# Recurrence gates from one stacked operand tile: a rounded half and its rest in the rows, both gates in the columns

## The chip, the cores and the metric

The kernel runs on one core of a Trainium2 chip. The metric is the device time of one execution in microseconds. Five engines work side by side, each through its own queue in order: TensorE (PE; its weight loads are shown apart as PEld), VectorE (DVE), ScalarE (ACT), GpSimd (POOL) and SyncE (SP), which issues the transfers here.

## What is computed

One layer of a hybrid decoder trunk on 2048 tokens of width 1024. A normalised input is projected to two groups that run side by side: four HGRN2 heads (a chunked gated recurrence with 128x128 states) and an RG-LRU group of width 512. Their outputs are concatenated, projected back and added to the input; a SwiGLU feed-forward part and a last norm follow. The part that the change touches is the RG-LRU group:

```python
def rglru_mix(xb, gate_b, conv_w, conv_b, wa, ba, wx, bx, a_param):
    ...
    xblk = xc.reshape(B, S, LRU_BLOCKS, LRU_BLOCK_DIM)
    r = jax.nn.sigmoid(jnp.einsum('bsnd,nde->bsne', xblk, wa.astype(jnp.float32)).reshape(B, S, W) + ba)
    ig = jax.nn.sigmoid(jnp.einsum('bsnd,nde->bsne', xblk, wx.astype(jnp.float32)).reshape(B, S, W) + bx)
    log_a = -LRU_C * r * jax.nn.softplus(-a_param.astype(jnp.float32))
    a = jnp.exp(log_a)
    b_in = jnp.sqrt(-jnp.expm1(2.0 * log_a)) * (ig * xc)
```

`xc` is the convolved input, 8 blocks of 64 channels. Both gates are block-diagonal: each block of 64 channels has its own 64x64 matrix in `wa` (recurrence gate `r`) and in `wx` (input gate `ig`).

## The kernel before

The sequence is worked in two halves of 1024 tokens, each in two blocks (`c` = 0, 1) of 512 tokens. Channels lie on the 128 partitions and tokens in the 512 columns. Large products run in a rounded 32-bit format; to keep the accuracy, both sides are split into a rounded part (`hi`, a ScalarE cast) and the rest (`lo`, a VectorE subtraction), and three matmuls hi·hi, lo·hi and hi·lo are added in PSUM (`feat_mm`, L234 to L236; `split`, L207 and L208).

After the values, a loop over eight steps `s` takes two weight slices and, for both blocks, makes two projections `pa` and `pb` of 24 matmuls each. Even steps feed one head of the HGRN2 group: `hg_pre` (`sf`, `lg`, `b`, the exponentials, the tiles `W`, `QI`, `K`), later `hg_mid` (transposes `pk`, scores `pc`), `hg_state` (`pu` and the four states `S`) and `hg_post` (`po`). Odd steps feed one unit of 128 channels, that is two blocks of 64, of the RG-LRU group: `lru_pre` (the convolution into `xc`, and its split `xh`, `xl`), then `lru_gates` (two PSUM banks `pr` and `pi`, three matmuls each against the gate weights `gwh` and `gwl`), then `lru_sigmoids` (`r`, `ig`, and the tanh `t`). The exponential, the root and the scan of a unit follow with the next even step's work (`exps`, `ends`). Names end in step and block: `pr_1_0` is the gate bank of step 1 (unit 0), block 0. The trace leaves these numbers out.

The gate weights are a 128x128 block-diagonal matrix for each unit and gate: half of its entries are zeros.

Two things set the order. Hooks in the loop (L1009 and on) place the later parts of a unit a number of projections behind; and the framework's scheduler then orders each engine's queue by a time line of its own. So small parts (`pk`, `pc`, `pu`, `po`, the gates) lie interleaved between the projections' matmuls on TensorE. A waiting instruction holds up all that stands behind it on its engine. There are four PSUM banks for projections and four for the small parts.

The feed-forward stage follows, with matmuls of 512 columns into `quad` banks and then the down projection.

Of the kernel before, what the change touches and what calls it, by code (L numbers as in the profile page):

```python
# [9 lines left out]
F32R = mybir.dt.float32r  # L10
# [8 lines left out]
NU = 4  # L19
# [9 lines left out]
NPAIR = NF // 2  # L29

C_LB0, C_LB1, C_CONVW, C_CONVB, C_BA, C_BX, C_A, C_NW, C_HN = 0, 4, 8, 24, 28, 32, 36, 40, 48
N_COLS = 49


@with_exitstack
def hybrid_layer(ctx: ExitStack, tc: tile.TileContext, x, x_t, norm_w, cols, w_in, gate_w, w_out, w_gu, w_down, out):
# [10 lines left out]
    def page(nm, dt=F32):  # L47
        return sb.tile([P, CW], dt, tag="pg", name=nm, bufs=16)
# [20 lines left out]
    def aux(nm):  # L69
        return psp.tile([P, CW], F32, tag="aux", name=nm)  # L70
# [192 lines left out]
    def table_act(out, in_, func, **kw):  # L263
        need = TABLES.get(func, at["table"])
        if need != at["table"]:
            in_line(lambda: nc.scalar.preload_act_table(func))
            at["table"] = need
        in_line(lambda: nc.scalar.activation(out=out, in_=in_, func=func, **kw))
# [145 lines left out]
    def lru_pre(u, psx, psg, nm):  # L414
        xp = sb.tile([P, CW + 4], F32, tag="pg", name="xp" + nm, bufs=16)
        v.tensor_copy(out=xp[:, 0:3], in_=hist[:, u, :])
        nc.scalar.copy(out=xp[:, 3 : 3 + CW], in_=psx)
        nc.gpsimd.tensor_copy(out=hist[:, u, :], in_=xp[:, CW : CW + 3])
        gl = page("gl" + nm)
        table_act(gl, psg, AF.Gelu_apprx_tanh)  # L420
        xc = page("xc" + nm)

        def cw(k):
            return par[:, C_CONVW + k * 4 + u : C_CONVW + k * 4 + u + 1]

        v.tensor_scalar(
            out=xc, in0=xp[:, 0:CW], scalar1=cw(0), scalar2=par[:, C_CONVB + u : C_CONVB + u + 1], op0=ALU.mult, op1=ALU.add
        )
        for k in range(1, 4):
            v.scalar_tensor_tensor(out=xc, in0=xp[:, k : k + CW], scalar=cw(k), in1=xc, op0=ALU.mult, op1=ALU.add)  # L430
        xh, xl = page("xh" + nm, dt=F32R), page("xl" + nm, dt=F32R)
        split((xh, xl), xc)
        return gl, xc, xh, xl


    def lru_gates(u, r, nm):
        gl, xc, xh, xl = r["pre"]
        r["p"] = pr, pi = aux("pr" + nm), aux("pi" + nm)
        for m, pg in enumerate((pr, pi)):
            gs = slice((m * NU + u) * P, (m * NU + u + 1) * P)  # L440
            nc.tensor.matmul(pg, lhsT=gwh[:, gs], rhs=xh, start=True, stop=False)
            nc.tensor.matmul(pg, lhsT=gwl[:, gs], rhs=xh, start=False, stop=False)
            nc.tensor.matmul(pg, lhsT=gwh[:, gs], rhs=xl, start=False, stop=True)

    def lru_sigmoids(u, d, nm):
        xc, (pr, pi) = d["pre"][1], d["p"]
        r, ig, t = d["r"] = xin("r" + nm), xin("ig" + nm), late("t" + nm)
        table_act(r, pr, AF.Sigmoid, bias=par[:, C_BA + u : C_BA + u + 1])
        table_act(ig, pi, AF.Sigmoid, bias=par[:, C_BX + u : C_BX + u + 1])
        table_act(t, r, AF.Tanh, scale=msp[:, u : u + 1])  # L450
        v.tensor_tensor(out=ig, in0=ig, in1=xc, op=ALU.mult)

# [720 lines left out]
def _layout(i):  # L1173
    import numpy as np

    a = {k: np.asarray(t) for k, t in i.items()}
    W = 512

    def by_rows(w):
        n = w.shape[1] // W  # L1180
        w = w.reshape(4, 2, P, n, W).transpose(3, 0, 2, 1, 4)
        return w.reshape(n * 4, P, D)

    def by_cols(w):
        n = w.shape[1] // P
        return w.reshape(KT, P, n, P).transpose(2, 1, 0, 3).reshape(n, P, D)

    w = a["w_in"][0]
    q, f_, v_, g_, lx, lg = (w[:, j * W : (j + 1) * W] for j in range(6))
    units = [by_rows(v_)]  # L1190
    for j in range(4):
        s = slice(j * P, (j + 1) * P)
        units += [by_cols(t[:, s]) for t in (q, f_, lx, lg)]
    units.append(by_rows(g_))

    def col(t):
        return t.reshape(-1, 4, P).transpose(2, 0, 1).reshape(P, -1)

    cols = [col(t) for t in (a["hg_lb"], a["conv_w"][0], a["conv_b"], a["lru_ba"], a["lru_bx"], a["lru_a"])]
    cols = np.concatenate(cols + [a["mix_norm_w"][0].reshape(KT, P).T, a["hg_norm_w"][0][:, None]], axis=1)  # L1200
    gate_w = np.zeros((P, 2, NU, P), np.float32)
    for m, t in enumerate((a["lru_wa"][0], a["lru_wx"][0])):
        for b in range(8):
            o = (b % 2) * 64
            gate_w[o : o + 64, m, b // 2, o : o + 64] = t[b]
    return {
        "x": a["x"][0],
        "x_t": a["x"][0].T,
        "norm_w": np.stack([a["mix_norm_w"][0], a["ffn_norm_w"][0], a["final_norm_w"]]),
        "cols": cols,  # L1210
        "w_in": np.concatenate(units, axis=0),
        "gate_w": gate_w.reshape(P, D),
        "w_out": by_rows(a["w_out"][0]),
        "w_gu": by_cols(a["w_gate_up"][0]),
        "w_down": a["w_down"][0].reshape(NF, P, D),
    }
# [19 lines left out]
```

## Time and profile before

| | us |
|---|---|
| median of 3 runs | 2115.37 |
| lowest and highest | 2114.73, 2115.42 |
| the profiled execution | 2114.84 |
| its span, first to last instruction | 2113.1 |

The profile is that of one execution. Its page gives the busy time of each engine and the chain of work that ended last; queries of its trace give groups of instructions, windows and a time line. TensorE's clock was granted at 0.999 over the span. What an engine that waits costs can be read only where TensorE or the last chain waits for it. By the windows the first 100 us hold 92.5 us of TensorE time, the window from 800 to 900 us 97.9, and all others up to 2100 us are full.

### The profile page before, as it was taken

The numbers are of one execution on the slowest core, as the hardware profiler recorded it, in microseconds if no ns is written. First come the engines' busy times: TensorE is split into PE (matmuls) and PEld (weight loads), VectorE is DVE, ScalarE is ACT, GpSimd is POOL, SyncE is SP. The second block draws the span as 40 slices with busy tenths as digits, with TensorE's granted clock in tenths as the row PEclk, the third lists the DMA queues.
The fourth block names the chain that finished last, engine by engine and source line by source line (L and its number), as shares of the span: only waits on it lengthen the run. The fifth ranks groups of instructions, "written<-read, shape, count | busy, mean of one in ns | idle before, by whom it ended". The sixth has DMA issues, their size and how long they took to land.

```text
span 2113.1 us, 26109 instructions
## 1 busy us (share of the span) xinstructions
PE 2096.0 (99%) x9704; PEld 1735.4 (82%) x9704; DVE 1485.9 (70%) x2415; ACT 959.0 (45%) x1608; POOL 77.0 (4%) x130
## 2 busy tenths in 40 slices
PE   8999999999999999999999999999999999999998
PEld 6888888888888887888888888888888888888887
DVE  5577765636777566877676669878867667669787
ACT  5566654535666554533333344335333333334333
POOL 2000001100000000000000000000000000000000
PEclk9999999999999999999999999999999999999999
DMA  5111115841111167423232266335423223267424
GB/s 210 51 41 41 41 40 183 293 140 52 39 33 40 42 224 233 152 93 125 95 109 97 89 238 217 120 133 189 145 95 130 95 95 110 95 222 247 155 85 145
DMA packets 138420, 262.84 MB, mean 124 GB/s; under 512 B 11186, under 2 KB 27570, under 8 KB 138292
## 3 DMA queue, kind: packets, MB, share of 16 engines
q1 hardware_dynamic: 138292, 261.17, 36.8%
q8 instruction: 76, 1.25, 0.2%
q14 instruction: 52, 0.43, 0.1%
HBM read 197.95 MB, written 63.18 MB: 124 GB/s over the span
## 4 chain that ended last, share of the span: by engine, by line
PE 97%; DMA 2%; DVE 1%; ACT 0%; issue 0%; SPq 0%; POOL 0%; DVEq 0%; POOLq 0%; ACTq 0%
PE quad_g L654 11%; PE quad_a L654 11%; PE quad_e L654 11%; PE pda L925 10%; PE pdb L925 7%; PE quad_f L654 6%; PE pb L235 3%; PE pb L236 3%; PE pa L235 3%; PE pa L234 3%; PE pa L236 3%; PE pb L234 3%; PE poh L246 2%; PE poh L247 2%; PE poh L248 2%; PE pg L248 1%
## 5 line engine op out<-in xcount | busy, mean ns | idle before, releaser
L654 PE MATMUL quad_f<-act_f,wgu_f 128*128 128x512 f32 x528 | 128.7, 393 | 1.9 <-ACT wgu_c L207 1.9
L654 PE MATMUL quad_a<-act_a,wgu_a 128*128 128x512 f32 x528 | 127.7, 390 | 0.2 <-DVE h L1114 0.2
L654 PE MATMUL quad_a<-act_b,wgu_b 128*128 128x512 f32 x528 | 127.1, 390 | 0.0
L654 PE MATMUL quad_g<-act_g,wgu_g 128*128 128x512 f32 x528 | 127.0, 390 | 0.0
L654 PE MATMUL quad_e<-act_e,wgu_e 128*128 128x512 f32 x528 | 126.9, 390 | 0.0
L654 PE MATMUL quad_e<-act_c,wgu_c 128*128 128x512 f32 x528 | 126.9, 390 | 0.0
L654 PE MATMUL quad_g<-act_d,wgu_d 128*128 128x512 f32 x528 | 126.8, 389 | 0.0
L654 PEld LDWEIGHTS quad_f<-act_f,wgu_f 128*128 128x128 f32 x528 | 100.2, 190 | 23.2 <-ACT act_g L207 2.3
L538 DVE TENSOR_TENSOR u<-u,quad_g 128x512 f32<-128x512 f32 x88 | 60.5, 688 | 79.7 <-PE quad_g L654 79.7
L654 PEld LDWEIGHTS quad_a<-act_a,wgu_a 128*128 128x128 f32 x528 | 98.9, 188 | 21.0 <-ACT act_c L207 0.6
L654 PEld LDWEIGHTS quad_e<-act_c,wgu_c 128*128 128x128 f32 x528 | 99.2, 188 | 20.6
L654 PEld LDWEIGHTS quad_g<-act_d,wgu_d 128*128 128x128 f32 x528 | 99.2, 188 | 20.5
L654 PEld LDWEIGHTS quad_g<-act_g,wgu_g 128*128 128x128 f32 x528 | 99.1, 188 | 20.5
L654 PEld LDWEIGHTS quad_e<-act_e,wgu_e 128*128 128x128 f32 x528 | 99.1, 188 | 20.5
L654 PEld LDWEIGHTS quad_a<-act_b,wgu_b 128*128 128x128 f32 x528 | 99.1, 188 | 20.5
L236 PE MATMUL pa<-xn,whi_in 128*128 128x512 f32 x256 | 100.9, 394 | 0.0
L234 PE MATMUL pa<-xn,whi_in 128*128 128x512 f32 x256 | 100.8, 394 | 0.0
L235 PE MATMUL pb<-xn,wlo_in 128*128 128x512 f32 x256 | 100.8, 394 | 0.0
L236 PE MATMUL pb<-xn,whi_in 128*128 128x512 f32 x256 | 100.7, 393 | 0.0
L235 PE MATMUL pa<-xn,wlo_in 128*128 128x512 f32 x256 | 100.5, 392 | 0.0
L234 PE MATMUL pb<-xn,whi_in 128*128 128x512 f32 x256 | 100.0, 391 | 0.0
L247 PE MATMUL poh<-wlo_o,mx 128*128 128x512 f32 x256 | 99.4, 393 | 0.0
(323 smaller groups left out, 4879.9 us busy)
## 6 DMA issues: line engine op xcount, KB each, us to landing
raw<-in_w_gu SPq DMA_DIRECT2D x88, 512.0 KB, 3.8
raw_in<-in_w_in SPq DMA_DIRECT2D x48, 512.0 KB, 3.5
ao_p<-as SPq DMA_DIRECT2D x76, 256.0 KB, 2.6
raw_o<-in_w_out SPq DMA_DIRECT2D x32, 512.0 KB, 4.1
x<-in_x SPq DMA_DIRECT2D x32, 256.0 KB, 5.7
xrh<-in_x SPq DMA_DIRECT2D x32, 256.0 KB, 3.6
h<-h SPq DMA_DIRECT2D x32, 256.0 KB, 3.4
hn<-hths SPq DMA_DIRECT2D x32, 256.0 KB, 3.7
```

Source lines behind the costliest of these rows:

```text
L234: nc.tensor.matmul(ps, lhsT=whi[:, ks], rhs=hi, start=(k == 0), stop=False)
L235: nc.tensor.matmul(ps, lhsT=wlo[:, ks], rhs=hi, start=False, stop=False)
L236: nc.tensor.matmul(ps, lhsT=whi[:, ks], rhs=lo, start=False, stop=(k == KT - 1))
L246: nc.tensor.matmul(ps, lhsT=hi, rhs=whi[:, ks], start=(k == 0), stop=False)
L247: nc.tensor.matmul(ps, lhsT=hi, rhs=wlo[:, ks], start=False, stop=False)
L248: nc.tensor.matmul(ps, lhsT=lo, rhs=whi[:, ks], start=False, stop=(k == KT - 1))
L538: (e or v).tensor_tensor(out=out, in0=a, in1=b, op=op)
L654: nc.tensor.matmul(ps, lhsT=w[:, s, ks], rhs=x, start=first and k + n == 0, stop=k == 3 and n == 2, skip_group_check=not first)
L925: nc.tensor.matmul(ps, lhsT=x, rhs=y, start=first and q + n == 0, stop=q == gr.n - 1 and n == 2, skip_group_check=not first)
```

## The change

A unit's 128 channels are two blocks of 64. The new `lru_pre` makes two operand tiles. In `za` rows 0 to 63 (`LO`) hold the rounded first block and rows 64 to 127 (`HI`) its rest; in `zb` rows 64 to 127 hold the rounded second block and rows 0 to 63 its rest. The gate weights are laid out anew: for each block of 64 channels the 64x64 matrices of both gates stand side by side in 128 columns, and the same 64 rows are repeated below. One matmul then multiplies the rounded part and the rest by the same weights and adds both, for both gates at once. With the rounded weights and with their rest this takes two matmuls a block of 64 channels, four a unit and token block, where six were. The products are those of before and one more (rest by rest).

Each PSUM bank now holds both gates of 64 channels, so `lru_sigmoids` empties it in halves: four sigmoids of 64 partitions in place of two of 128. For `ig` the result goes to the other half of the partitions; four more parameter columns hold `bx` with its halves exchanged. The two casts and two subtractions of `lru_pre` work on 64 partitions each, and the subtractions write to the other half.

```diff
+C_BXS = 49
+N_COLS = 53
+LO, HI = slice(0, P // 2), slice(P // 2, P)
...
-        xh, xl = page("xh" + nm, dt=F32R), page("xl" + nm, dt=F32R)
-        split((xh, xl), xc)
-        return gl, xc, xh, xl
+        z = page("za" + nm, dt=F32R), page("zb" + nm, dt=F32R)
+        for t, here, there in ((z[0], LO, HI), (z[1], HI, LO)):
+            nc.scalar.copy(out=t[here], in_=xc[here])
+            v.tensor_tensor(out=t[there], in0=xc[here], in1=f(t[here]), op=ALU.subtract)
+        return gl, xc, z
...
     def lru_gates(u, r, nm):
-        gl, xc, xh, xl = r["pre"]
-        r["p"] = pr, pi = aux("pr" + nm), aux("pi" + nm)
-        for m, pg in enumerate((pr, pi)):
-            gs = slice((m * NU + u) * P, (m * NU + u + 1) * P)
-            nc.tensor.matmul(pg, lhsT=gwh[:, gs], rhs=xh, start=True, stop=False)
-            nc.tensor.matmul(pg, lhsT=gwl[:, gs], rhs=xh, start=False, stop=False)
-            nc.tensor.matmul(pg, lhsT=gwh[:, gs], rhs=xl, start=False, stop=True)
+        r["p"] = aux("pr" + nm), aux("pi" + nm)
+        for b, (pg, z) in enumerate(zip(r["p"], r["pre"][2])):
+            gs = slice((2 * u + b) * P, (2 * u + b + 1) * P)
+            nc.tensor.matmul(pg, lhsT=gwh[:, gs], rhs=z, start=True, stop=False)
+            nc.tensor.matmul(pg, lhsT=gwl[:, gs], rhs=z, start=False, stop=True)
 
     def lru_sigmoids(u, d, nm):
-        xc, (pr, pi) = d["pre"][1], d["p"]
+        xc, (pa, pb) = d["pre"][1], d["p"]
         r, ig, t = d["r"] = xin("r" + nm), xin("ig" + nm), late("t" + nm)
-        table_act(r, pr, AF.Sigmoid, bias=par[:, C_BA + u : C_BA + u + 1])
-        table_act(ig, pi, AF.Sigmoid, bias=par[:, C_BX + u : C_BX + u + 1])
+        for dst, c0, to, ps, at_ in ((r, C_BA, LO, pa, LO), (r, C_BA, HI, pb, HI), (ig, C_BXS, LO, pa, HI), (ig, C_BXS, HI, pb, LO)):
+            table_act(dst[to], ps[at_], AF.Sigmoid, bias=par[at_, c0 + u : c0 + u + 1])
         table_act(t, r, AF.Tanh, scale=msp[:, u : u + 1])
...
-    gate_w = np.zeros((P, 2, NU, P), np.float32)
...
+    wa, wx = a["lru_wa"][0], a["lru_wx"][0]
+    gate_w = np.concatenate([np.concatenate([wa[b], wx[b]] if b % 2 == 0 else [wx[b], wa[b]], axis=1) for b in range(8)], axis=1)
+    gate_w = np.concatenate([gate_w, gate_w], axis=0)
```

The scheduler orders the queues anew around the gates. Three places of the first half show how; the second half has the same pieces. Line numbers are those of the kernel before and of the changed kernel.

TensorE, the gates of unit 0, block 1 (`pr_1_1`, `pi_1_1`), between the matmuls of the next step's projection `pb_2_0`. Before, from the seventh matmul of that projection on:

```order
L234 MATMUL pb_2_0_1172<-xn_0_00_162,whi_in_9_894 128x512
L441 MATMUL pr_1_1_1161<-xh_1_1_1112,gw 128x512
L442 MATMUL pr_1_1_1161<-xh_1_1_1112,gw 128x512
L441 MATMUL pi_1_1_1162<-xh_1_1_1112,gw 128x512
L442 MATMUL pi_1_1_1162<-xh_1_1_1112,gw 128x512
L235 MATMUL pb_2_0_1172<-xn_0_00_162,wlo_in_9_895 128x512
L236 MATMUL pb_2_0_1172<-xn_0_10_164,whi_in_9_894 128x512
L234 MATMUL pb_2_0_1172<-xn_0_00_162,whi_in_9_894 128x512
L443 MATMUL pr_1_1_1161<-xl_1_1_1113,gw 128x512
L443 MATMUL pi_1_1_1162<-xl_1_1_1113,gw 128x512
```

In the changed kernel, from its seventeenth matmul on:

```order
L237 MATMUL pb_2_0_1174<-xn_0_01_163,wlo_in_9_895 128x512
L238 MATMUL pb_2_0_1174<-xn_0_11_165,whi_in_9_894 128x512
L444 MATMUL pr_1_1_1165<-za_1_1_1112,gw 128x512
L445 MATMUL pr_1_1_1165<-za_1_1_1112,gw 128x512
L236 MATMUL pb_2_0_1174<-xn_0_01_163,whi_in_9_894 128x512
L444 MATMUL pi_1_1_1166<-zb_1_1_1113,gw 128x512
L445 MATMUL pi_1_1_1166<-zb_1_1_1113,gw 128x512
```

Six gate matmuls became four, and the last of them moved from behind the tenth matmul of `pb_2_0` to behind the nineteenth.

ScalarE, the same gates' sigmoids and the forget gate `sf_2_0` of the next step, which empties `pb_2_0`. Before:

```order
L268 ACTIVATE sq_2_0_1169<-pa_2_0_1128 128x512
L268 ACTIVATE r_1_1_1197<-pr_1_1_1161,par 128x512
L268 ACTIVATE ig_1_1_1198<-pi_1_1_1162,par 128x512
L268 ACTIVATE t_1_1_1199<-r_1_1_1197,tinies 128x512
L268 ACTIVATE sf_2_0_1204<-pb_2_0_1172 128x512
```

In the changed kernel:

```order
L270 ACTIVATE sq_2_0_1171<-pa_2_0_1130 128x512
L270 ACTIVATE r_1_1_1199<-pr_1_1_1165,par 64x512
L270 ACTIVATE r_1_1_1199<-pi_1_1_1166,par 64x512
L270 ACTIVATE ig_1_1_1200<-pr_1_1_1165,par 64x512
L270 ACTIVATE ig_1_1_1200<-pi_1_1_1166,par 64x512
L270 ACTIVATE t_1_1_1201<-r_1_1_1199,tinies 128x512
L270 ACTIVATE sf_2_0_1208<-pb_2_0_1174 128x512
```

Four half sigmoids stand ahead of `sf_2_0` where two whole ones stood; three of them read `pi` or stand behind one that does.

VectorE, the states `S_2_0` of the second head and block 0, which the output products `po` read, and the operand subtractions of unit 1. Before:

```order
L388 SCALAR_TENSOR_TENSOR S_2_0_1418<-carry,G_2_0_1224,pu_2_0_1413 128x128
L388 SCALAR_TENSOR_TENSOR S_2_0_1418<-S_2_0_1418,G_2_0_1224,pu_2_0_1413 128x128
L208 TENSOR_TENSOR xl_3_0_1502<-xc_3_0_1496,xh_3_0_1501 128x512
L416 COPY xp_3_1_1591<-hist 128x3
L388 SCALAR_TENSOR_TENSOR S_2_0_1418<-S_2_0_1418,G_2_0_1224,pu_2_0_1413 128x128
L164 TENSOR_TENSOR wlo_in_14_1609<-raw_in_14_1606,whi_in_14_1608 128x1024
```

In the changed kernel:

```order
L390 SCALAR_TENSOR_TENSOR S_2_0_1422<-carry,G_2_0_1228,pu_2_0_1417 128x128
L166 TENSOR_TENSOR wlo_in_14_1615<-raw_in_14_1612,whi_in_14_1614 128x1024
L418 COPY xp_3_1_1595<-hist 128x3
L390 SCALAR_TENSOR_TENSOR S_2_0_1422<-S_2_0_1422,G_2_0_1228,pu_2_0_1417 128x128
L436 TENSOR_TENSOR za_3_0_1505<-xc_3_0_1500,za_3_0_1505 64x512
L390 SCALAR_TENSOR_TENSOR S_2_0_1422<-S_2_0_1422,G_2_0_1228,pu_2_0_1417 128x128
L436 TENSOR_TENSOR zb_3_0_1506<-xc_3_0_1500,zb_3_0_1506 64x512
```

A weight slice's subtraction moved from behind the third state to ahead of the second, and the one operand subtraction became two, before and behind the third state.

SyncE's and GpSimd's queues hold the same instructions in the same order, with a parameter transfer of 53 columns instead of 49.

More of the change, by code (lines that the diff above doesn't have):

```diff
@@ L31 @@
 C_LB0, C_LB1, C_CONVW, C_CONVB, C_BA, C_BX, C_A, C_NW, C_HN = 0, 4, 8, 24, 28, 32, 36, 40, 48
-N_COLS = 49
+C_BXS = 49
+N_COLS = 53
+LO, HI = slice(0, P // 2), slice(P // 2, P)
 @with_exitstack
@@ L1200, in _layout @@
     cols = np.concatenate(cols + [a["mix_norm_w"][0].reshape(KT, P).T, a["hg_norm_w"][0][:, None]], axis=1)
-    gate_w = np.zeros((P, 2, NU, P), np.float32)
[L1202 to L1205, printed above, removed]
+    bx = col(a["lru_bx"])
+    cols = np.concatenate([cols, np.concatenate([bx[64:], bx[:64]], axis=0)], axis=1)
+    wa, wx = a["lru_wa"][0], a["lru_wx"][0]
+    gate_w = np.concatenate([np.concatenate([wa[b], wx[b]] if b % 2 == 0 else [wx[b], wa[b]], axis=1) for b in range(8)], axis=1)
+    gate_w = np.concatenate([gate_w, gate_w], axis=0)
     return {
@@ L1211, in _layout @@
         "w_in": np.concatenate(units, axis=0),
-        "gate_w": gate_w.reshape(P, D),
+        "gate_w": gate_w,
         "w_out": by_rows(a["w_out"][0]),
```

## The prediction

> **What bounds the kernel now.** I read the page first, for the span and the engine that is always busy.
>
> ```profile
> span 2113.1 us, 26109 instructions
> PE 2096.0 (99%) x9704; PEld 1735.4 (82%) x9704; DVE 1485.9 (70%) x2415; ACT 959.0 (45%) x1608; POOL 77.0 (4%) x130
> PE 97%; DMA 2%; DVE 1%; ACT 0%; issue 0%; SPq 0%; POOL 0%; DVEq 0%; POOLq 0%; ACTq 0%
> ```
>
> The third line is the chain of waits that ended last: 97% of the span is TensorE working, and VectorE's share is 1%, DMA's 2%. Busy time alone would not prove that, since matmuls overlap in the records. So I then read the busy time by windows: first the two stretches in which the recurrence gates run (one for each half of the sequence), then a stretch of the feed-forward stage, where nothing but 512-column matmuls runs. The columns are the window, its length, busy time and instruction count of TensorE, of its weight loads, of VectorE, ScalarE and GpSimd, the granted clock, DMA share and GB/s.
>
> ```profile
> 100.00:320.00 220.00, 220.00 (x1151) 183.73 (x1150) 153.69 (x337) 136.75 (x247) 15.98 (x23) 1.00 0.12 39
> 560.00:760.00 200.00, 200.00 (x1032) 166.84 (x1030) 138.84 (x296) 118.12 (x211) 11.88 (x18) 1.00 0.17 54
> 1000.00:1100.00 100.00, 100.00 (x443) 82.86 (x442) 67.84 (x103) 35.02 (x59) 0.00 (x0) 1.00 0.27 90
> ```
>
> In the gate stretches TensorE is never idle, at full granted clock, with DMA at 0.12 and 0.17. The last row gives the price of a 512-column matmul in a full stream: 100 us / 443 = 0.226 us. Time there is a count of matmuls times a step. The groups by line show that the gates' matmuls wait for nothing (the last figure of a row is the idle time before them):
>
> ```profile
> L443 PE MATMUL pi<-xl,gw 128*128 128x512 f32 x16 | 6.3, 394 | 0.0
> L443 PE MATMUL pr<-xl,gw 128*128 128x512 f32 x16 | 6.3, 393 | 0.0
> ```
>
> **What the change removes.** Each of 2 halves x 4 units x 2 blocks = 16 gate groups falls from six 128x512 matmuls to four: 32 fewer. The tempting price is 0.393 us, the mean of one in these rows; it is wrong, because matmuls overlap. The timeline shows one undisturbed group (start, duration, instruction):
>
> ```profile
> 177.85 0.40 PE L441 MATMUL pr<-xh,gw 128*128 128x512 f32 x1
> 178.09 0.39 PE L442 MATMUL pr<-xh,gw 128*128 128x512 f32 x1
> 178.31 0.39 PE L443 MATMUL pr<-xl,gw 128*128 128x512 f32 x1
> 178.54 0.39 PE L441 MATMUL pi<-xh,gw 128*128 128x512 f32 x1
> 178.77 0.39 PE L442 MATMUL pi<-xh,gw 128*128 128x512 f32 x1
> 179.00 0.40 PE L443 MATMUL pi<-xl,gw 128*128 128x512 f32 x1
> 179.24 0.39 PE L234 MATMUL pb<-xn,whi_in 128*128 128x512 f32 x1
> ```
>
> From 177.85 to 179.24 six matmuls take 1.39 us, 0.232 us each start to start. Two fewer save 0.463 us, and 16 groups 7.4 us. With the feed-forward step of 0.226 it is 7.2 us; those are the ends of this term.
>
> Here a page is weighed. The Trainium skill (TensorE: Matmul & The Clock Gate, Back-to-back issue gap) puts a 512-column matmul of a sustained load-and-multiply stream at about 131 ns; by it the saving would be 32 x 0.131 = 4.2 us. The 0.232 us of this trace disagrees, and the measurement decides.
>
> **What it adds, and what hides it.** ScalarE gets one cast and two sigmoids more per group, VectorE one subtraction, all on 64 partitions and some writing to the other half of the partitions. No row of the trace has that form. The whole-tile forms are:
>
> ```profile
> L207 ACT CAST xh<-xc x16: 609/620/652, 101.5 to 693.1; 128x512 fp32r<-128x512 f32 x16
> L208 DVE TENSOR_TENSOR xl<-xc,xh x16: 682/685/693, 102.1 to 694.0; 128x512 fp32r<-128x512 f32 x16
> L268 ACT ACTIVATE r<-pr,par x16: 687/689/713, 117.7 to 702.1; 128x512 f32<-128x512 f32 x16
> L268 ACT ACTIVATE ig<-pi,par x16: 680/688/722, 118.3 to 702.7; 128x512 f32<-128x512 f32 x16
> ```
>
> Does half the partitions cost half? The nearest rows set 32 partitions against 128 at an equal 128 columns, first on ScalarE, then on VectorE:
>
> ```profile
> 158.52 0.26 ACT L374 COPY sct<-pc 32x128 f32<-32x128 f32 x1 [1.09 <-DVE sct L372]
> 164.24 0.28 ACT L406 ACTIVATE ojk<-po 128x128 f32<-128x128 f32 x1 [2.76 <-PE po L401]
> 154.37 0.28 DVE L372 COPY_PREDICATED sct<-keep,pc 32x128 f32<-32x128 uint8 x1
> 155.10 0.27 DVE L342 TENSOR_TENSOR lg<-lg,G 128x128 f32<-128x128 f32 x1
> ```
>
> The time goes by columns, not by partitions. I take full price: ScalarE 16 x (0.62 + 2 x 0.69) = 32.0 us, VectorE 16 x 0.69 = 11.0 us. From below the halves would cost half and ScalarE and VectorE would gain nothing and lose nothing; the upper end, with writing across halves at double price, is 16 x (4 x 1.38 + 2 x 1.24 - 2 x 0.69 - 0.62) = 96 us on ScalarE. The cover is in the window rows: in 420 us ScalarE is busy 136.75 + 118.12 = 254.9 us and VectorE 153.69 + 138.84 = 292.5, so even 96 us more leaves ScalarE under 351 of 420. What matters is where they stand in their queues. Three places:
>
> *The gates' own operands.* For the group above the operands were made here:
>
> ```profile
> 173.17 0.61 ACT L207 CAST xh<-xc 128x512 fp32r<-128x512 f32 x1
> 173.98 0.69 DVE L208 TENSOR_TENSOR xl<-xc,xh 128x512 fp32r<-128x512 f32 x1
> ```
>
> The rest ended at 174.67, and its first reader started at 178.31: 3.6 us early. A second cast and subtraction put the second tile back by 0.62 + 0.69 = 1.3 us, and the new order sets the gates later in the stream. About 2.3 us are left. Cost: none.
>
> *ScalarE between the gates and the next unit's forget gate.* Behind the sigmoids stand `t` and then `sf`, which starts the long chain to the key tile `lg`:
>
> ```profile
> 125.92 0.69 ACT L268 ACTIVATE r<-pr,par 128x512 f32<-128x512 f32 x1 [2.85 <-PE pr L443]
> 126.50 0.68 ACT L268 ACTIVATE ig<-pi,par 128x512 f32<-128x512 f32 x1
> 127.07 0.72 ACT L268 ACTIVATE t<-r,tinies 128x512 f32<-128x512 f32 x1
> 129.41 0.60 ACT L268 ACTIVATE sf<-pb 128x512 f32<-128x512 f32 x1 [1.61 <-PE pb L236]
> 145.62 0.42 DVE L339 TENSOR_TENSOR lg<-nx,G 128x256 f32<-128x256 f32 x1
> 150.01 0.60 PE L352 MATMUL pk<-ident,lg 128*128 128x128 f32 x4
> ```
>
> By the new order the last gate matmul has 19 matmuls of `pb` before it instead of 10 and two gate matmuls less: 9 x 0.227 - 2 x 0.232 = 1.58 us later from `pb`'s start, and `pb` ends 0.46 earlier, so 2.04 us closer to its end. Two more sigmoids follow it, at their pitch of 0.58 (126.50 - 125.92), 1.16. Of these 3.2 us, 1.61 us fill the idle time before `sf`, so `sf` slips by about 1.6 us. Its chain ended at 146.04, 4.0 us before the transposes `pk`, and the new order sets those four matmuls (0.9 us) later: 3.3 us stay. Cost: none. Were the cover gone, each pair of blocks would pay the slip itself, 8 x 1.6 = 13 us.
>
> *VectorE's state chain in unit 1, block 0.* A weight subtraction and the operand subtractions now stand between the states:
>
> ```profile
> 160.97 0.34 DVE L388 SCALAR_TENSOR_TENSOR S<-S,G,pu 128x128 f32<-128x128 f32 x1
> 161.22 1.22 DVE L164 TENSOR_TENSOR wlo_in<-raw_in,whi_in 128x1024 fp32r<-128x1024 f32 x1
> 163.59 0.39 PE L400 MATMUL po<-S,QI 128*128 128x128 f32 x2
> ```
>
> The last state ended at 161.31, 2.28 us before TensorE read it. The 1.22 us subtraction before it takes about that away, and two `pb` matmuls moved ahead of the reader give 0.46 back: some 1.5 us stay. Cost: none.
>
> No transfer is added or moved: the queues of SyncE and GpSimd stand as before, with a parameter transfer four columns wider ahead of the first gates. TensorE's order is the same up to the first gate group, and after the last region of gates it is the same again, so the later stages move up whole.
>
> **Sum.** The profiled execution took 2114.84 us (1.7 us of it around the span); 2114.84 - 7.4 = 2107.4. The median shown is 2115.37, 0.5 us above it, so I predict 2107.9.
>
> **Rivals.**
>
> *Operands or sigmoids late (within 0.2%).* TensorE works in order; a gate matmul that waits stops the projection behind it. Against it: the margins above, 1.5 to 3.3 us. For it: they are computed across an order that changed on three engines, and cross-half writes are unseen. A stall of 0.3 us in each group gives back 16 x 0.3 = 4.8 of 7.4: 2112.8 us. The Trainium skill (TensorEngine Tiling (Array Packing), PSUM Bottleneck) warns of this, that a faster TensorE leaves the emptying of PSUM as the limit, and advises sharing it between ScalarE and VectorE. Here all of it stays on ScalarE.
>
> *The saving is given back at the handover (no change).* Between projection and feed-forward TensorE does wait:
>
> ```profile
> L654 PE MATMUL quad_f<-act_f,wgu_f 128*128 128x512 f32 x528 | 128.7, 393 | 1.9 <-ACT wgu_c L207 1.9
> 800.00:900.00 100.00, 97.87 (x437) 79.87 (x436) 80.95 (x131) 47.82 (x92) 3.94 (x4) 0.98 0.58 187
> ```
>
> If transfers alone set that moment, 7.4 us saved before it would come back as idle time there: 2115. Against it: the DMA engines are 0.58 busy in that window, not full, and the weight slices loaded there take buffers that come free when TensorE has read the slices before them, so they follow it.
>
> *ScalarE's queue becomes the bound (slower).* Place: the sigmoids ahead of `sf`, once in each of 8 pairs of blocks. Three half sigmoids remain there behind the last gate matmul. The slip of 1.6 us grows by three times whatever one costs above its 0.58 pitch, 3.3 us of it are free, and to lose all 7.4 us each pair must stall 0.93 us. That needs (3.3 + 0.93) / 3 = 1.4 us more, a half sigmoid of 2.0 us. At 2.3 us the stalls are 8 x (3 x 1.72 - 3.3) = 15 us and the time 2123. The 32-partition rows speak against it.
>
> *A removed matmul is worth less than its step (within 0.2%).* If the stream closed up behind it only in part, because the load of its weights and the start of the next matmul had overlapped it, the least it can be worth is the step of a matmul with a quarter of the columns:
>
> ```profile
> 156.67 1.05 PE L383 MATMUL pu<-v,kut 128*128 128x128 f32 x8
> 157.56 0.39 PE L400 MATMUL po<-carry,QI 128*128 128x128 f32 x2
> ```
>
> Eight in 0.89 us are 0.11 us each, so 32 x 0.11 = 3.5 us and 2115.37 - 3.5 = 2111.9. The feed-forward row of 443 matmuls in 100 us speaks against it: there too each loads its own weights, and the stream does not close up further. The Trainium skill's 131 ns, weighed above, lies between the two prices.
>
> **How the numbers follow.** Forecast 0.85; late operands 0.07; handover 0.03; the cheaper step 0.02; ScalarE's queue 0.03. A measurement of this kernel tells about 0.2%, 4.2 us, from no change, so faster means below 2111.1: 0.85. Within 0.2% are the late operands, the handover and the cheaper step, 0.12; slower is 0.03. The forecast's own range is 7.2 to 7.4 us saved, 0.6 us between profile and median, and about 1 us of wobble where transfers meet the start and the handover: 2106.5 to 2109. I stretch it towards the small stalls, to 2111, and to 2105.8 below.
>
> **What would show it.** Right: 32 fewer matmuls on TensorE, still 100% busy in the gate stretches, gates' idle time 0.0, ScalarE's busy time up by about 32 us and VectorE's by 11, half sigmoids near 0.69 us, and the handover some 7 us earlier. Wrong: idle time of TensorE released by ScalarE or VectorE before the gates, `pk` or `po`; half-tile rows well over 0.7 us; or a longer wait at `quad_f`.

## The result, and the profile after

| | before | changed | ratio, 95% interval |
|---|---|---|---|
| median (19 runs each), us | 2116.28 | 2111.04 | 0.9977 [0.9971, 0.9984] |
| lowest and highest, us | 2112.43, 2118.24 | 2108.14, 2113.41 | |

The change makes the kernel 5.2 us faster. The forecast was 7.4 us less and a time of 2107.9 us. Timed again beside other kernels, the gain was 4.0, 3.9 and 4.4 us.

The page of the changed kernel, its span, busy times and chain of waits:

```profile
span 2108.1 us, 26128 instructions
PE 2088.5 (99%) x9672; PEld 1727.5 (82%) x9672; DVE 1499.7 (71%) x2431; ACT 995.1 (47%) x1656; POOL 74.6 (4%) x130
PE 92%; DMA 3%; DVE 3%; issue 1%; ACT 0%; POOL 0%; SPq 0%; DVEq 0%; POOLq 0%; ACTq 0%
```

TensorE has the 32 matmuls fewer, and its busy time fell by 7.5 us. But TensorE's share of the chain fell too, from 97% to 92%: in this profile more of the chain runs through waits for DMA (2% before, 3% now) and through VectorE (1% and 3%). ScalarE is busy for 36.1 us more, VectorE for 13.8.

The windows that were shown of before, now of the changed kernel:

```profile
100.00:320.00 220.00, 220.00 (x1151) 183.50 (x1150) 161.74 (x347) 154.55 (x271) 14.18 (x23) 1.00 0.12 39
560.00:760.00 200.00, 200.00 (x1025) 166.55 (x1025) 146.85 (x300) 133.25 (x230) 10.13 (x18) 1.00 0.19 60
800.00:900.00 100.00, 98.03 (x444) 79.58 (x443) 82.17 (x134) 48.82 (x93) 3.94 (x4) 1.00 0.53 173
```

TensorE is still never idle in the gate stretches, and the handover window holds no more idle time than before (1.97 us against 2.13). The groups of the gate matmuls, then those of three half-tile operations, then three half sigmoids in the time line:

```profile
L444 PE MATMUL pr<-za,gw 128*128 128x512 f32 x16 | 7.0, 436 | 0.0
L445 PE MATMUL pr<-za,gw 128*128 128x512 f32 x16 | 6.3, 395 | 0.0
```

```profile
L435 ACT CAST za<-xc x16: 606/621/622, 101.9 to 690.1; 64x512 fp32r<-64x512 f32 x16
L436 DVE TENSOR_TENSOR za<-xc,za x16: 684/685/689, 102.6 to 690.8; 64x512 fp32r<-64x512 f32 x16
L270 ACT ACTIVATE ig<-pi,par x16: 681/682/684, 120.2 to 700.0; 64x512 f32<-64x512 f32 x16
```

```profile
118.12 0.68 ACT L270 ACTIVATE r<-pr,par 64x512 f32<-64x512 f32 x1
118.82 0.69 ACT L270 ACTIVATE r<-pi,par 64x512 f32<-64x512 f32 x1
119.53 0.69 ACT L270 ACTIVATE ig<-pr,par 64x512 f32<-64x512 f32 x1
```

No gate matmul waits. Work on half the partitions costs the full price (0.62, 0.685 and 0.682 us against 0.620, 0.685 and 0.688), across halves or not; and the half sigmoids start 0.70 us apart, where whole ones started 0.58 apart.

**Where the time went.** Some matmuls mark the same point of the work in every profile: the last into `pv` (values), `pg` (output gate) and `poh` (output projection) of each half of the sequence, and the first and last into `pd` (down projection). They cut TensorE's time line into stages. A gate stretch runs from the last `pv` of a half to its last `pg`. Its ends in the first half, of before and then of the changed kernel:

```profile
62.85 0.39 PE L248 MATMUL pv<-whi_in,xn 128*128 128x512 f32 x1
330.06 0.39 PE L248 MATMUL pg<-whi_in,xn 128*128 128x512 f32 x1
```

```profile
63.27 0.39 PE L250 MATMUL pv<-whi_in,xn 128*128 128x512 f32 x1
327.22 0.39 PE L250 MATMUL pg<-whi_in,xn 128*128 128x512 f32 x1
```

That is 267.21 and 263.95 us. With the further profiles told below, the stages are these (means, us):

| stage on TensorE | before (3 profiles) | changed (4) | difference |
|---|---|---|---|
| start to the last `pv` of half 0 | 63.21 | 63.57 | +0.36 |
| gate stretch of half 0 | 267.21 | 263.95 | -3.25 |
| to the last `poh` of half 0 | 95.14 | 95.12 | -0.02 |
| to the last `pv` of half 1 | 47.18 | 47.18 | 0.00 |
| gate stretch of half 1 | 267.17 | 264.05 | -3.11 |
| to the last `poh` of half 1 | 92.65 | 92.82 | +0.17 |
| to the first `pd` | 579.40 | 579.23 | -0.17 |
| first `pd` to last `pd` | 65.86 | 67.65 | +1.79 |
| to the last matmul | 628.32 | 628.32 | 0.00 |

In sum TensorE's last matmul starts 4.24 us earlier. The gate stretches are the same in every profile of a kernel to 0.02 us, so a difference of 0.3 us there is real. They give 6.37 us, not 7.4; and 1.79 us is lost again in the stage of `pd`, 700 us behind the last gate.

Inside a stretch I gave each matmul the time to the next one's start and summed by tile. The gates fall from 11.76 to 8.03 us in half 0, -3.73, and by 3.69 in half 1: 7.42 us in all, as forecast. Against that, 1.05 us are given back, 0.86 of them by the small matmuls `pc` (0.30) and `po` (0.56) and 0.15 by `pg`. In the time line of step 2 (the second head), block 1, before:

```profile
161.92 0.39 PE L401 MATMUL po<-v,sct 128*128 128x128 f32 x2
162.23 0.43 PE L360 MATMUL pc<-W,nx 128*64 128x128 f32 x2
162.59 0.49 PE L400 MATMUL po<-S,QI 128*128 128x128 f32 x2
162.92 0.39 PE L401 MATMUL po<-v,sct 128*128 128x128 f32 x2
163.14 0.39 PE L400 MATMUL po<-S,QI 128*128 128x128 f32 x2
```

and in the changed kernel:

```profile
161.83 0.39 PE L403 MATMUL po<-v,sct 128*128 128x128 f32 x2
162.15 0.32 PE L362 MATMUL pc<-W,nx 128*64 128x128 f32 x1
...
162.51 0.49 PE L402 MATMUL po<-S,QI 128*128 128x128 f32 x2
162.84 0.39 PE L403 MATMUL po<-v,sct 128*128 128x128 f32 x2
163.15 0.32 PE L362 MATMUL pc<-W,nx 128*64 128x128 f32 x1
...
163.73 0.49 PE L402 MATMUL po<-S,QI 128*128 128x128 f32 x2
```

`pc` multiplies with 64 columns of weights (`128*64`), `po` with 128. Two `po` in a row take 0.22 us (162.92 to 163.14); where a `pc` follows, 0.31 (161.92 to 162.23), and where a `pc` came before, 0.33 (162.59 to 162.92). A change of tile alone does not do it: the last `pu` ahead of a `po`, both with 128 columns, takes the 0.11 us of the others (the prediction's rows at 156.67 and 157.56). A run is a row of `pc` with no other matmul between. Before, the eight `pc` of this block came in two runs, 1 + 7; now they come in three, 2 + 3 + 3. Over the program there are 22 such runs before and 24 now. The new order on TensorE did it; no engine waits.

### The profile page after: what moved, and what is told of

Its sections match the earlier page's. It is cut to its first block, busy times and chain, and to the rows that moved or that the text cites. A ratio compares the mean times of both kernels' runs of the same rounds, so it can differ in the third digit from the quotient of the medians.

```text
span 2108.1 us, 26128 instructions
## 1 busy us (share of the span) xinstructions
PE 2088.5 (99%) x9672; PEld 1727.5 (82%) x9672; DVE 1499.7 (71%) x2431; ACT 995.1 (47%) x1656; POOL 74.6 (4%) x130
## 3 DMA queue, kind: packets, MB, share of 16 engines
q8 instruction: 76, 1.25, 0.2%
## 4 chain that ended last, share of the span: by engine, by line
PE 92%; DMA 3%; DVE 3%; issue 1%; ACT 0%; POOL 0%; SPq 0%; DVEq 0%; POOLq 0%; ACTq 0%
PE quad_e L656 11%; PE quad_g L656 11%; PE quad_a L656 11%; PE pda L927 10%; PE pdb L927 6%; PE quad_f L656 6%; PE pb L238 3%; PE pb L237 3%; PE pa L236 3%; PE pb L236 3%; PE pa L237 3%; PE pa L238 3%; PE poh L249 2%; PE poh L248 2%; PE poh L250 2%; PE pg L248 1%
```

## The experiments

**The same kernels again.** No edit.

> The changed kernel once more, for its waits. In its first profile each gate stretch (from the last matmul into pv to the last into pg) took 263.95 us in the first half and 264.05 in the second, against 267.2 before, and TensorE waited outside the stretches at 398 us (0.62 us), at 848 and 852 us (0.6 each) and at 1437 us (1.6 us), where the kernel before did not. Theory A (order and transfers): the stretches are a matter of order and come out the same to 0.1 us, while the waits outside them come from transfers that land later or earlier in each execution, so that they stand elsewhere this time. Theory B (late operands): the added work on ScalarE and VectorE makes those waits, and they stand at the same places with the same length.

2111.47 us, 0.9977 [0.9968, 0.9986]; stretches 263.95 and 264.05, so the order sets them. Outside, both theories have a part: the wait near 398 us did not come back, while those near 850 us stood again and that near 1437 us was longer.

> The kernel before, unchanged, profiled once more. Disputed: whether the TensorE waits at about 400 us (0.8 us), 850 us (two of 0.6 us) and 1440 us (1.4 to 3.1 us), which stand in all five profiles of rearranged kernels and not in the first profile of before, belong to the rearrangement. Theory 'the feed-forward's loads land earlier or later from one execution to the next': at least one of two new profiles of before has a wait of 1 to 3 us near 1440 us, and its span is longer than 2113.1 us by about that. Rival 'the rearrangement causes them': neither profile has a TensorE wait over 0.3 us near 1440 us, and both spans are 2112.6 to 2113.8 us. By both, the two stretches from the last pv to the last pg take 267.2 us each, as before.

> The same kernel as before_look1, a second profile, with the same expectations: under 'loads land earlier or later' a wait near 1440 us in at least one of the two and spans that differ by over 1 us; under 'the rearrangement causes them' no such wait in either and spans that agree within 1 us.

The spans were 2113.6 and 2115.3 us (time 2115.33 and 2117.03), the stretches 267.21 and 267.17. TensorE waited near 1440 us in both (steps of 0.73 and 1.25 us from one start to the next, where 0.23 is usual; 1.81 and 3.10 in the first two profiles of the changed kernel), and at 400 and 850 us too. So these waits belong to before as well; the first profile, on which the prediction rests, had happened to miss them. But the wait near 1440 is longer after the change.

**The halves alone**: before, with the casts, subtractions and sigmoids done on 64 partitions, and six matmuls a group.

```diff
-        split((xh, xl), xc)
+        for rows in (slice(0, P // 2), slice(P // 2, P)):
+            split((xh[rows], xl[rows]), xc[rows])
...
-        table_act(r, pr, AF.Sigmoid, bias=par[:, C_BA + u : C_BA + u + 1])
-        table_act(ig, pi, AF.Sigmoid, bias=par[:, C_BX + u : C_BX + u + 1])
+        for dst, ps, c0 in ((r, pr, C_BA), (ig, pi, C_BX)):
+            for rows in (slice(0, P // 2), slice(P // 2, P)):
+                table_act(dst[rows], ps[rows], AF.Sigmoid, bias=par[rows, c0 + u : c0 + u + 1])
```

> The kernel before with its six gate matmuls, its casts, rests and sigmoids of the gates cut into two halves of 64 partitions: 64 small instructions more on ScalarE (32 us) and 16 more on VectorE, no matmul saved. Theory A: this work is hidden; the order gets 24 visits of TensorE to the 64-column score matmuls instead of 22, at 0.34 us each, so the stretches take 267.5 us and the time rises by 0.7 us, within noise. Theory B: the work costs the 2 to 3 us that the change fell short of its forecast, as idle time of TensorE released by ScalarE or VectorE.

> halves_only once more: its profile had a span of 2113.6 us, 4 us under what its timed median of 2119.2 us allows for, so that profile did not show where the half-tile operations cost time. Theory 'the halves cost TensorE nothing but the extra runs of 64-column matmuls': stretches of 267.75 and 267.61 us again, and what is longer in this profile stands outside them, in the start, the handovers near 400 and 840 us or the stage of pd. Rival 'the halves make TensorE wait in the gate stretches in most executions': stretches over 268.5 us here.

2119.24 us, 1.0018 [1.0009, 1.0027]: the halves alone cost 3.8 us (48 instructions more on ScalarE and 16 on VectorE; the expectation's 64 is their sum). The stretches are 267.75 and 267.61, +0.98 in all, with 24 runs of `pc` as in the changed kernel: the extra runs come from the half-tile operations, not from the missing matmuls. The first profile was 4 us short of the median; the second (span 2118.1 us, the same stretches) has the rest outside: against the mean of before +1.45 and +0.60 us in the two output projections (`poh`), +1.05 in the stage of `pd`. Why these waits come more often here is open.

**Fewer runs of `pc`**: the score matmuls are held behind the last `po` before them, in the changed kernel (`chain_after`) and in before (`chain_before`); `hold_two` does it in the changed kernel for the second block of the heads of steps 4 and 6 alone ("units 2 and 3" in its expectation; some expectations call a run a visit).

```diff
+                with tc.issue_after(last_po[0]) if ... else nullcontext():
                     nc.tensor.matmul(pc[...], ...)
...
-            nc.tensor.matmul(po[:, ns], lhsT=sc[:, n, :], ...)
+            last_po[0] = nc.tensor.matmul(po[:, ns], lhsT=sc[:, n, :], ...).ins
```

> The changed kernel with the score matmuls pc held behind the last output matmul po, so that each of the 16 groups of eight pc is one visit instead of 24 visits in all. Theory A: each visit costs 0.34 us, so a stretch takes 263.95 - 4 x 0.34 = 262.6 us, 2.7 us less in all, and the kernel is 7.5 to 8 us faster than before. Rival: the mixing of pc and po costs nothing by itself, the pieces only move; the stretches stay at 264, or rise where po or the next projection waits.

> The kernel before with the same hold: 16 visits instead of 22. Theory A: a stretch takes 267.2 - 3 x 0.34 = 266.2 us, 2 us less in all. Against the held changed kernel the difference in a stretch is then the gate matmuls alone, 16 x 0.232 = 3.7 us. If a removed gate matmul were worth less than its step of 0.232 us (0.11 us at least), that difference would be 1.8 us.

> The changed kernel with the score matmuls of the second block of units 2 and 3 held behind the last output matmul of the first block, so that the 64-column matmuls come in 20 runs in place of 24 (10 a half in place of 12). Theory 'each run of 64-column matmuls among 128-column ones costs about 0.34 us': each stretch from the last pv to the last pg falls from 263.95 and 264.05 to about 263.3 us, and the time by some 1.4 us, to about 2109.7 us with the same waits outside. Rival 'the hold delays the gated output as in chain_after': a TensorE wait of about 2 us before pg at 308 and 715 us, stretches of 264.5 us or more, and 2111 to 2113 us. Rival 'the runs cost nothing': stretches of 263.9 to 264.1 us.

| | runs of `pc` | stretches, us | time, us | ratio to before |
|---|---|---|---|---|
| before | 22 | 267.21, 267.17 | | |
| chain_before | 16 | 266.19, 266.13 | 2114.71 | 0.9993 [0.9985, 1.0002] |
| changed | 24 | 263.95, 264.05 | 2111.04 | 0.9977 [0.9971, 0.9984] |
| hold_two | 20 | 263.24, 263.34 | 2110.54 | 0.9973 [0.9963, 0.9983] |
| chain_after | 16 | 264.51, 264.62 | 2113.03 | 0.9986 [0.9977, 0.9995] |

Six runs fewer give 2.06 us in before, four fewer 1.42 in the changed kernel: 0.34 and 0.36 us each. So the two extra runs of the change cost about 0.7 of its 1.05 us. By tile, `pc` and `po` take 0.43 us for each run in all three pairs (2.58 us for six, 1.72 for four, 0.86 for the change's two), and in the held kernels other matmuls take up to 0.1 us a run of that back. (The halves alone have 0.69 for their two.) What is left of the 1.05, mostly in `pg`, has no shown cause. In time alone `hold_two` can't be told from the changed kernel.

In `chain_after` the gain is eaten by a wait. The waits of TensorE in its first gate stretch, then in that of `two_matmuls` (below):

```profile
PE pg L248 <- ACT sg L270: 1.6, 1, 1.6
```

```profile
PE pg L248 <- ACT sg L270: 3.4, 1, 3.4
```

The wait also spoils the comparison that the expectation of `chain_before` set up. The stretches of the two held kernels differ by 1.68 and 1.51 us, near the 1.8 of a matmul worth 0.11 us; but by tile the gates differ by 3.48 and 3.52 us, 0.22 us for each matmul.

**Another 32 matmuls fewer**: the changed kernel with two matmuls a group of gates in place of four. It leaves out the products with the rest of the gate weights.

```diff
-            nc.tensor.matmul(pg, lhsT=gwh[:, gs], rhs=z, start=True, stop=False)
-            nc.tensor.matmul(pg, lhsT=gwl[:, gs], rhs=z, start=False, stop=True)
+            nc.tensor.matmul(pg, lhsT=gwh[:, gs], rhs=z, start=True, stop=True)
```

> The changed kernel without the products with the rest of the gate weights (two matmuls a unit and block in place of four; that part of the product is left out), so another 32 fewer of the same shape; its 64-column matmuls come in 18 runs in place of 24. Theory 'a gate matmul is worth its full step': each stretch falls by 16 x 0.232 = 3.7 us for the matmuls and 3 x 0.34 = 1.0 us for the runs, to 259.2 and 259.3 us; of the 9.4 us in all about the same part as in the change is lost outside, so the time falls by 7 to 9.4 us below the changed kernel's, to about 2102 to 2104 us. Rival 'a removed matmul is worth half its step (0.11 us)': stretches of 261.1 us and about 2106 to 2108 us. Rival 'ScalarE or VectorE now set the pace of the gate stretch': stretches over 262 us with TensorE waits over 1 us in them.

2114.05 us, 0.9991 [0.9982, 1.0000]: some 3 us slower than the changed kernel. The gates did give 3.9 us a half; but the stretches are 264.67 and 264.75, because `pg` takes 5.3 us a half more. The third theory is borne out, at the end of the stretch. ScalarE's time line there in this kernel, and then in the changed one:

```profile
305.73 0.63 ACT L270 ACTIVATE t<-t 128x512 f32<-128x512 f32 x1
306.38 1.28 ACT L268 ACT_TABLE_LOAD   x1
307.67 1.58 ACT L270 ACTIVATE sg<-pg 128x512 f32<-128x512 f32 x3
```

```profile
298.95 1.23 ACT L270 ACTIVATE t<-t 128x512 f32<-128x512 f32 x2
300.20 1.28 ACT L268 ACT_TABLE_LOAD   x1
301.49 1.09 ACT L270 ACTIVATE sg<-pg 128x512 f32<-128x512 f32 x2
```

The sigmoids that empty `pg` stand in ScalarE's queue behind the last unit's roots `t` and a table load. In the changed kernel they start at 301.49; here at 307.67, while TensorE came to need the bank at 304.7. So further savings run into ScalarE's queue at the last unit. How much of these 6.2 us is the chain itself is not shown: the new order also put two pieces of the output's work (`mx`, 303.59 and 304.70) ahead of the last root, 1.6 us, where the changed kernel has them behind `sg`.

**The instruction fetch.** The wait near 1440 us, in the stage of `pd`, is for VectorE. Its row in the changed kernel:

```profile
PE pd L794 <- DVE hd L540: 1.4, 1, 1.4
```

VectorE had stood idle some 12 us earlier, for ScalarE, and ScalarE for a load of `b`. VectorE's rows in before and in the changed kernel, then ScalarE's:

```profile
1431.51 0.69 DVE L208 TENSOR_TENSOR act_a<-b,act_a 128x512 fp32r<-128x512 f32 x1 [0.86 <-ACT act_a L207]
1426.47 0.69 DVE L210 TENSOR_TENSOR act_a<-b,act_a 128x512 fp32r<-128x512 f32 x1 [2.57 <-ACT act_a L209]
```

```profile
1430.86 0.62 ACT L207 CAST act_a<-b 128x512 fp32r<-128x512 f32 x1 [1.89 <-DMA b<-hn]
```

```profile
1425.82 0.62 ACT L209 CAST act_a<-b 128x512 fp32r<-128x512 f32 x1 [3.60 <-DMA b<-hn]
```

From that operation to `hd` VectorE works without a gap. (The profile's chain of the changed kernel goes by another load there, `raw_d`, which lands 0.02 us before VectorE's next operation, on `b`, starts; in before that operation starts 1.0 us ahead of the landing, so it does not wait for it.) SyncE's order of transfers is the same in both. The DMA view of the eight us around this load, before first (queue q1 alone: packets, MB, share; then the load's KB and us to landing), then the changed kernel:

```profile
q1 hardware_dynamic: 452, 1.34, 51.4%
b<-hn SPq DMA_DIRECT2D x1, 256.0 KB, 3.1
```

```profile
q8 instruction: 1, 0.02, 1.1%
b<-hn SPq DMA_DIRECT2D x1, 256.0 KB, 4.8
```

In the changed kernel one packet of 16 KB was under way on q8, an instruction fetch. There are 76 in the span, one per 256 instructions of TensorE (9672 matmuls, as many weight loads and 112 others, by 256); with fewer instructions in `two_matmuls` there are 75, with more in `pad_before` (below) 77. The one in question comes after some 13,470 to 13,490 of them in every kernel but the two paddings of before, where it is the next one, 256 later. The changed kernel has 48 fewer ahead of it (32 matmuls and 32 loads fewer, 16 semaphore instructions more; the expectations say 64), so the fetch falls 5 to 8 us later in the work. To move it without the change, small matmuls are put ahead of everything; their result is overwritten. Each of the 16 below is two matmuls and two loads on TensorE; `pad_before` has 48 and `pad_before2` 52.

```diff
+                dot = const.tile([1, 1], F32, name="dot")
+                v.memset(dot, 1.0)
+                for _ in range(16):
+                    nc.tensor.matmul(wmix[0][0:1, 0:1], lhsT=dot, rhs=dot, start=True, stop=True)
                 for n in range(2):
                     nc.tensor.matmul(wmix[n], lhsT=one, rhs=wrow[n][0:1, :], start=True, stop=True)
```

> The changed kernel with 32 more TensorE matmuls (one element by one element, with their 32 weight loads; their result is overwritten) put ahead of everything, where TensorE has nothing to do until 4.05 us: as many TensorE instructions as the kernel before has, and nothing else moved. Disputed: why the stage from the first pd to the last pd takes 66.9 and 68.4 us in the two profiles of the changed kernel and 65.4, 65.8 and 66.3 us in the three of before. Theory 'the fetch of TensorE's instructions': a 16 KB transfer comes once for each 256 TensorE instructions; with 64 fewer of them it has moved from 11.4-11.7 us to 17.8-19.5 us after the first pd, onto the load of b that ScalarE waits for, which lands in 4.5 to 4.8 us in place of 3.1 to 3.7. So here the fetch stands at 10 to 13 us after the first pd again, that load lands in 3.1 to 3.8 us, the stage takes 65.4 to 66.6 us, and the time falls by about 1.2 us against the changed kernel. Rival 'the new arrays or the earlier arrival of the stage': the load still lands in 4.4 us or more and the stage takes 66.8 us or more.

> pad_after again, beside its own second profile: its one profile had the fetch 11.8 us after the first pd, the load of b landing in 2.9 us and a stage of 65.5 us, but its timed median, 2111.8 us, was only 0.3 us below that of the changed kernel beside it. Theory 'the fetch costs the stage of pd about 1.1 us, and its other places cost or save what hides that in the time': fetch at 10 to 13 us, that load in 2.8 to 3.8 us, stage 65.4 to 66.6 us again, time 2110 to 2112 us. Rival 'the short stage was chance': the load lands in 4.4 us or more, or the stage takes 66.8 us or more with the load at 3.5 us.

> A further profile of the same kernel, same expectations: under the theory fetch at 10 to 13 us after the first pd, load of b in 2.8 to 3.8 us, stage 65.4 to 66.6 us; under 'chance' a stage of 66.8 us or more in at least one of pad_after2 and pad_after3.

> The changed kernel unchanged, beside the padded ones on the same chip. Under 'the fetch of TensorE's instructions': a 16 KB fetch 17 to 20 us after the first pd, the load of b on it lands in 4.4 us or more, the stage takes 66.8 us or more. Under 'loads land early or late by chance' the landing lies anywhere between 3 and 5 us. Stretches 263.95 and 264.05 us by both; a ratio to before of 0.997 to 0.998.

> The kernel before with 96 small matmuls and their loads ahead, 192 TensorE instructions: three quarters of a 16 KB fetch, so that the next fetch stands where the changed kernel has it. Theory 'the fetch of TensorE's instructions': a fetch 17 to 20 us after the first pd, the load of b lands in 4.4 us or more, and the stage from the first pd to the last takes 66.7 us or more though nothing of the change is in the kernel. Rival 'the new arrays or the earlier arrival': the load lands in 3.1 to 3.8 us and the stage takes 65.4 to 66.4 us. Stretches of 267.2 us by both; the start is later by up to 8 us, since the small matmuls don't fit into TensorE's idle time there.

> The kernel before with 104 small matmuls ahead in place of 96: in pad_before the fetch stood at 19.2 us, 0.6 us before the load of b, issued at 16.6 us, had landed (3.2 us), so it missed it. 16 more TensorE instructions bring the fetch some 1.8 us forward, to about 17.4 us. Theory 'the fetch delays the load that it falls on': that load lands in 4.3 us or more, and the stage of pd takes 66.7 us or more, in a kernel without the change. Rival 'the long landing belongs to the changed kernel's arrays or arrival': it lands in 3.1 to 3.8 us. Stretches of 267.1 us by both.

Times in us after the first `pd`, for all 20 profiles of this study; "takes" is the load of `b`, from issue to landing:

| profiles | fetch starts | load issued | takes | stage of `pd` |
|---|---|---|---|---|
| before, its two looks | 11.4-11.7 | 16.3-16.6 | 3.1, 3.4, 3.7 | 65.4, 65.8, 66.3 |
| chain_before, halves_only, halves_again | 11.0-11.6 | 16.9-17.8 | 3.4, 3.5, 3.0 | 66.8, 66.5, 66.9 |
| pad_after, pad_after2, pad_after3 | 10.8-11.8 | 16.0-17.3 | 2.9, 3.5, 3.3 | 65.5, 65.6, 67.1 |
| pad_hold, pad_hold2 | 11.2, 12.0 | 17.7, 16.6 | 3.2, 3.1 | 67.2, 66.2 |
| two_matmuls | 27.7 | 18.0 | 3.5 | 67.7 |
| pad_before | 19.2 | 16.6 | 3.2 | 65.9 |
| pad_before2 | 18.8 | 16.3 | 5.0 | 68.8 |
| changed, its three repeats | 16.9-19.5 | 16.0-17.8 | 4.8, 4.5, 4.8, 4.4 | 66.9, 68.4, 68.0, 67.3 |
| hold_two, chain_after | 18.2, 18.6 | 16.1, 16.4 | 4.6, 4.6 | 66.8, 67.2 |

Where the fetch lies on the load, it takes 4.4 to 5.0 us; where it doesn't, 2.9 to 3.7. The padding takes the fetch and the long landing away from the changed kernel, and `pad_before2`, in a single profile, brings both into before. `pad_before` missed its aim: its fetch came only 0.6 us before the landing, and the load took 3.2 us. The stage takes 67.6 us on the mean of the seven with the fetch and 66.4 on that of the thirteen without: 1.2 us. It also varies by 2 us for other reasons (`pad_after3`, `pad_hold`: an earlier load took 5.5 us). The padding shortens the two gate stretches too, by 0.34 us in the changed kernel (263.82 and 263.84) and some 0.17 in before; the cause is not shown.

The time does not show it clearly: `pad_after` took 2111.78 us, 0.9978 [0.9969, 0.9987], beside 2112.07 for the changed kernel; `pad_after2` 2109.29, 0.9969 [0.9957, 0.9981].

**Both together**: `hold_two` with the small matmuls.

> hold_two with the same 32 small matmuls ahead. If both mechanisms are right they add: stretches of 263.24 and 263.34 us, a stage of pd of 65.4 to 66.6 us, and a time some 1.4 + 1.2 us below the changed kernel's, about 2108.5 us and a ratio to before of 0.9965 or less. If the fetch is not the cause, the ratio is that of hold_two, 0.9973, and the stage takes 66.8 us or more.

> pad_hold once more, beside the changed kernel on the same chip. If both mechanisms are right, its median lies 1.4 to 2.6 us below that of after_last; if the fetch brings nothing to the time, 1.4 us at most; if neither does, the two agree within 0.5 us. The stage of pd has no certain value here: in pad_hold it was 67.2 us with the load of b landing in 3.2 us, because an earlier load took 5.5 us.

> The changed kernel beside pad_hold2: 2110.5 to 2112.5 us, a fetch 16 to 20 us after the first pd, the load of b under it landing in 4.4 us or more (theory of the fetch) or anywhere from 3 to 5 us (chance).

2108.51 us, 0.9965 [0.9953, 0.9978], and 2109.10 us, 0.9968 [0.9956, 0.9980]; the changed kernel beside them 0.9983 [0.9974, 0.9992] and 0.9982 [0.9973, 0.9991], 3.6 and 2.2 us slower. This version is the fastest of the study. The intervals of the ratios overlap, but run by run the difference is plain: its twelve executions took 2106.0 to 2109.6 us, the 22 of the changed kernel beside them 2109.5 to 2115.9.

## Why the prediction was wrong

*The saving term* was right: 32 matmuls at 0.232 us, 7.4 forecast, 7.42 measured by tile, and against `halves_only`, which has the same halves and six matmuls, the changed kernel is 7.8 us faster, 7.36 of them in the gate stretches. The rival of a cheaper matmul (0.11 us) falls with it. That its 2111.9 us came nearest to the measured 2111.0 is chance: what it describes did not happen. The 131 ns that the Trainium skill (TensorE: Matmul & The Clock Gate, Back-to-back issue gap) gives do not hold in this kernel either.

*The price of the half-tile operations* was right per operation: full price, and VectorE's 13.8 us against 11.0, ScalarE's 36.1 against 32.0. The pitch of 0.58 us taken for half sigmoids was 0.70, so four halves add 1.6 us ahead of `sf`, not 1.16. The margin there was wide enough: none of the three places examined waited (the gates, `pk` and `po` all have 0.0 idle time), and "late operands" did not happen.

*"Cost: none" is the step that failed*, together with "No transfer is added or moved" and "after the last region of gates it is the same again, so the later stages move up whole". All of them looked for an engine that waits because it is late, at places picked from the order; the sum has no term for what the new order costs TensorE itself, and none for a transfer that the program does not issue. The halves cost 3.8 us when tried alone, and at none of these places. Two mechanisms were shown: the scheduler's new order, which the half-tile operations brought, cut `pc` into more runs, and these cost TensorE time with no idle row (about 0.7 us of the 1.05 given back in the stretches); and TensorE's fewer instructions moved an instruction fetch onto a load that ScalarE waits for, 700 us behind the last gate (about 1.2 of the 1.79 us in the stage of `pd`). The rest of the 3.8 us of the halves stays open. The start (+0.36) and the rest of that stage vary between profiles by as much as they differ. Also, one profile of before was taken for its usual course, though its stage of `pd` had no wait, and two further profiles had one.

*The handover* gave nothing back: the stage up to the first `pd` is 0.17 us shorter, and the step with the wait at `quad_f` takes 1.9 us on the mean of before and 2.0 on that of the changed kernel.

*ScalarE's queue as the bound* did not happen in the change, but `two_matmuls` and `chain_after` show that it was near, at another place than the one named: not the sigmoids ahead of `sf` but the work ahead of the last `sg`.

## What to carry to other kernels

Price removed matmuls by their step, but then compare the new order for how often TensorE changes its weight-tile shape: a change cost time here that no wait showed. Work done at an engine with 50% idle time can still cost, through the order that a scheduler makes of it. Cut several profiles of a kernel into stages at fixed landmarks before trusting a wait's absence; and test a second saving of the same kind before counting on it, since the first may have used up the cover.

## What the runs showed of the hardware

A run of 64-column matmuls among 128-column ones costs 0.34 to 0.36 us in the two pairs of kernels above. The Trainium skill (TensorEngine Tiling (Array Packing), Key Properties) says that a change of tiling mode drains TensorE. The trace does not show the mode, but it agrees in the step from a 128-column matmul to a 64-column one, 0.20 us in place of 0.11.

TensorE's instruction fetch is a DMA transfer beside the kernel's loads: where its 16 KB fell on a 256 KB load, the load landed some 1.4 us later (4.7 us against 3.3 on the means). The Trainium skill (Runtime: NRT & Kernel Launch, Instruction fetch mechanics) gives the blocks of 256 instructions, with which the 76 fetches agree, and calls the cost mostly hidden. No row here has TensorE waiting for a fetch, but a load that another engine waits for came later by it.

After TensorE's wait of 3.4 us in `two_matmuls` (3.8 from start to start) its clock was lower for a while. Windows of the wait and of the 3.7 us behind it:

```profile
304.50:308.32 3.82, 0.39 (x2) 0.00 (x1) 3.82 (x6) 3.79 (x7) 0.56 (x1) 1.00 0.00 0
308.32:312.00 3.68, 3.68 (x10) 2.86 (x11) 3.68 (x6) 2.43 (x5) 0.89 (x1) 0.56 0.41 143
```

The granted clock fell to 0.56, and about ten matmuls ran in the time of sixteen (3.68 / 0.227): the wait cost 1.4 us more than it lasted. The length of the wait does not decide it alone. In the first profile of before the clock fell to 0.59 over the 3.7 us behind the wait at `quad_f` (2.26 us from start to start), while it stayed at 1.00 behind the 3.10 us near 1438 us in the changed kernel's second profile.
